# The seven-product form for all eight chunk pairs of an up group, and one panel of the down rounds added up in its banks

## The chip, the cores and the metric

One core of one Trainium2 chip runs the kernel. The metric is device time in microseconds (us) of one execution. The engines of the core work side by side and wait for each other by semaphores: TensorE (PE, matmuls; PEld is its loading of stationary operands), VectorE (DVE), ScalarE (ACT), GpSimd (POOL) and SyncE (SP). SP and POOL issue DMAs, each in the order of its own program. On the chip matmuls write into eight PSUM banks; here a bank holds a tile of 128 rows and 512 columns.

## What is computed

One layer of a streaming encoder for 256 frames of a new stream and 8 x 16 frames of running streams: 384 tokens, in three tiles of 128 (tiles 0 and 1 are the new stream, tile 2 the running ones). The change concerns the last part, the feed-forward block:

```python
h2 = rmsnorm(x, norm_ffn_g)
up = h2 @ w_up                       # 2048 -> 2 x 5632
g_half, u_half = up[..., :D_FF], up[..., D_FF:]
ext_f = concatenate([ffn_buf, g_half], axis=1)
gc = causal_dwconv(ext_f, ffn_dw_w, ffn_dw_b)      # 3 taps along the frames
x = x + (silu(gc) * u_half) @ w_down               # 5632 -> 2048
new_ffn = ext_f[:, -2:]
```

All inputs and outputs are float32.

## The kernel before

Each float32 operand of a matmul is split into a high half (a copy rounded to the matmul's type, made by ACT: `hi`) and a low half (the rest, a subtraction on DVE: `lo`). A product of a 128 x 128 block of tokens and a 128 x 512 block of weights is three matmuls into one bank: high by high, high by low, low by high (`three`). The tokens are the stationary operand. The weights come by SP as loads of 512 KB, two chunks of 128 rows by 512 columns each, into streaming buffers (`raw`, and `raws`, two more in a tile that is free by then: five in all).

Up to the output projection the program runs in `gemm`. The feed-forward part goes by `FFN_PLAN`: 11 groups of 512 columns of the inner width. An up group g makes the gate and value rows of its columns; a down round multiplies the group's activation into four panels of 512 output columns, 2 steps of 18 matmuls each, and adds each panel's three banks into `y` on DVE. Up group g+1 runs ahead of the down round of group g. Group 0 is plain (`plain_up`, 288 matmuls). Groups 1 to 10 run in `wino`, with 16 chunks of the 2048 inputs taken as 8 pairs. For a pair with chunks c0 and c1, tokens x0 (tile 0) and x1 (tile 1), gate weights G0, G1 and value weights U0, U1, the eight products of the 2 x 2 block product are done as seven, with four combinations of tokens (`sums`, made once per layer) and four of weights, made on DVE for every pair:

- S1 = U0 - G0, S2 = U0 - U1, S3 = U1 - S1, S4 = G1 - S3

Tile 2 takes four plain products, with one sum of tokens so that it can share S2. That is 11 products a pair in place of 12. In the kernel before, pairs 0 to 5 run so and pairs 6 and 7 (chunks 12 to 15) run plainly: 6 x 11 + 2 x 12 = 90 products. The steps (`WINO_STEPS`) are "s" (gate weights as loaded, 12 matmuls), "b" (the U1 of two pairs, 12 matmuls), "t" (the combined weights, two splits with 9 and 6 matmuls; gate and value weights of the pair are loaded for it, the gate weights a second time), and "cg", "cu" (plain pairs, 18 matmuls): 270 matmuls, 25 splits and 25 loads a group.

The order of the work around a step is set by a planner inside the program, when the program is built. `step` puts down one step: it issues ACT's high half of the split that is next in `staged`, the row work that the step before released (`fins`), the matmuls, the low half on DVE, and the sums for the next pair (`combine`). Row work of earlier groups waits in `todo` and is put down by `work` whenever the planner's clock (`now`, with a cost per operation) says that an engine has time. The engines then run exactly that order. Two splits are prepared ahead of the step that PE works on (`ready`), in three pairs of tiles.

`finish_up` is the row work of a group: gate and value rows come out of the banks (`rows_from` on ACT, `rows_plus` on DVE), are turned in blocks (DVE, into `tb`), moved by SP and POOL into `uT`, and then run through the conv taps (`sg`), SiLU and product into the split activation `act`. `norm_panel`, ahead of the feed-forward part, turns and splits the normalized tokens into `xg` and makes the `sums`.

## Time and profile before

| | |
|---|---|
| three timed runs, median (lowest to highest) | 1957.12 us (1957.06 to 1957.96) |
| the profiled execution | 1957.32 us, its span 1955.6 us |
| granted clock of TensorE | 1.00 |
| feed-forward part | from 908.2 us to the end |
| HBM read | 314 MB, 165 GB/s over the span with the writes |

A row of the timeline has the start and the duration in us, the engine, the line of the program, the operation, what it writes and reads with its shape, and a count; in brackets stands the idle time of the engine in front of it and what ended that. All calls that the planner issues for DVE, ACT, POOL and SP have one line, that of a helper (L1112), so such rows are told apart by their tiles. A row of the groups by line has count, busy time in all, mean duration in ns, idle time in front and what ended it.

### The profile page before, as it was taken

Reading aid. Unit: us, or ns where it says so; the run is one execution under the profiler, and the core shown is the slowest. Engines: PE = TensorE matmul, PEld = TensorE weight load, DVE = VectorE, ACT = ScalarE, POOL = GpSimd, SP = SyncE. Lnnn points to the kernel's source line nnn. Section 1 sums busy time; section 2 is a strip of 40 time slices with the busy share of each in tenths; the row PEclk is TensorE's granted clock in tenths of the full one; section 3 lists DMA queues with packets and bytes.
Section 4 is the critical chain, followed back from the end, with each engine's and each line's share of the span. In section 5 each row is a group of like instructions: output and inputs, shape, how many; then the busy total and the mean of one; then the engine's idle time right before and its main releaser. Section 6 shows DMA issues by size and latency. Waiting matters only on the chain.

```text
span 1955.6 us, 25545 instructions
## 1 busy us (share of the span) xinstructions
PE 1945.8 (99%) x9192; PEld 1639.0 (84%) x9192; DVE 1478.2 (76%) x2016; ACT 878.3 (45%) x1220; POOL 150.8 (8%) x298
## 2 busy tenths in 40 slices
PE   9999999999999999999999999999999999999999
PEld 9888999988888888888888888888887888888887
DVE  4456979888764578677587878787878787878885
ACT  5535454433333523344454444454444444454552
POOL 2000011100000000000111010101010101010110
PEclk9999999999999999999999999999999999999999
DMA  6574777554444333644576666666666666667664
GB/s 188 149 184 118 221 169 154 146 141 134 131 131 126 122 129 119 201 133 139 155 218 203 198 203 200 201 203 197 207 191 205 195 213 191 207 192 217 209 185 141
DMA packets 245203, 340.58 MB, mean 174 GB/s; under 512 B 60794, under 2 KB 106549, under 8 KB 245067
## 3 DMA queue, kind: packets, MB, share of 16 engines
q1 hardware_dynamic: 237875, 328.93, 56.9%
q0 software_dynamic: 7168, 10.00, 1.9%
q8 instruction: 72, 1.18, 0.3%
q14 instruction: 56, 0.46, 0.1%
q10 hardware_dynamic: 32, 0.01, 0.0%
HBM read 314.17 MB, written 7.86 MB: 165 GB/s over the span
## 4 chain that ended last, share of the span: by engine, by line
PE 93%; DVE 4%; issue 1%; ACT 1%; DMA 1%; SPq 0%; ACTq 0%; DVEq 0%
PE bank L1368 16%; PE bank L1369 16%; PE bank L1367 16%; PE acc L325 8%; PE acc L323 8%; PE acc L324 8%; PE misc L325 4%; PE misc L323 4%; PE misc L324 4%; PE acc L318 2%; PE acc L320 2%; PE acc L319 2%; DVE lo L1112 1%; DVE raw L1112 1%; ACT hi L1112 1%
## 5 line engine op out<-in xcount | busy, mean ns | idle before, releaser
L175 DVE TENSOR_TENSOR lo<-raw,hi 128x1024 fp32r<-128x1024 f32 (+2 forms) x219 | 259.9, 1188 | 196.1 <-ACT hi L174 193.9
L174 ACT CAST hi<-raw 128x1024 fp32r<-128x1024 f32 (+2 forms) x219 | 221.6, 1012 | 391.6 <-PE misc L325 305.4
L1112 ACT CAST hi<-raw 128x1024 fp32r<-128x1024 f32 x215 | 225.7, 1050 | 319.7 <-PE bank L1369 268.9
L1112 DVE TENSOR_TENSOR lo<-raw,hi 128x1024 fp32r<-128x1024 f32 x215 | 262.0, 1221 | 86.4 <-ACT hi L1112 83.2
L1368 PE MATMUL bank<-lo,xg 128*128 128x512 f32 x656 | 256.4, 391 | 1.6 <-DVE lo L1112 1.6
L1367 PE MATMUL bank<-hi,xg 128*128 128x512 f32 x656 | 255.3, 389 | 0.0
L1369 PE MATMUL bank<-hi,xg 128*128 128x512 f32 x656 | 255.3, 389 | 0.0
L1112 ACT CAST hi<-raws 128x1024 fp32r<-128x1024 f32 x137 | 144.4, 1054 | 201.6 <-PE bank L1369 166.4
L1112 DVE TENSOR_TENSOR lo<-raws,hi 128x1024 fp32r<-128x1024 f32 x137 | 167.3, 1222 | 64.4 <-ACT hi L1112 62.2
L1368 PE MATMUL bank<-lo,act 128*128 128x512 f32 x528 | 205.6, 389 | 0.0
L1369 PE MATMUL bank<-hi,act 128*128 128x512 f32 x528 | 205.4, 389 | 0.0
L1367 PE MATMUL bank<-hi,act 128*128 128x512 f32 x528 | 205.4, 389 | 0.0
L323 PE MATMUL acc<-hi,hT 128*128 128x512 f32 (+1 forms) x512 | 192.9, 377 | 0.0
L325 PE MATMUL acc<-hi,hT 128*128 128x512 f32 (+1 forms) x512 | 190.4, 372 | 0.1
L324 PE MATMUL acc<-lo,hT 128*128 128x512 f32 (+1 forms) x512 | 190.3, 372 | 0.2 <-DVE lo L175 0.2
L840 DVE SCALAR_TENSOR_TENSOR ut<-ext,cw,ut 128x384 f32<-128x384 f32 x240 | 151.3, 630 | 6.0
L1368 PEld LDWEIGHTS bank<-lo,xg 128*128 128x128 f32 x656 | 123.1, 188 | 31.0 <-DVE lo L1112 5.8
L1112 POOL DMA_DIRECT2D uT<-tb x168 | 82.8, 500 | 855.5 <-DVE y L1112 640.7
L1367 PEld LDWEIGHTS bank<-hi,xg 128*128 128x128 f32 x656 | 123.1, 188 | 25.9
L1369 PEld LDWEIGHTS bank<-hi,xg 128*128 128x128 f32 x656 | 123.2, 188 | 25.3
L1368 PEld LDWEIGHTS bank<-lo,act 128*128 128x128 f32 x528 | 99.1, 188 | 21.1 <-DVE lo L1112 0.6
L1367 PEld LDWEIGHTS bank<-hi,act 128*128 128x128 f32 x528 | 99.1, 188 | 20.6
(355 smaller groups left out, 3620.2 us busy)
## 6 DMA issues: line engine op xcount, KB each, us to landing
raw<-in_w_up_dram SPq DMA_DIRECT2D x161, 512.0 KB
raws<-in_w_up_dram SPq DMA_DIRECT2D x105, 512.0 KB
raw<-in_w_in_dram SPq DMA_DIRECT2D x96, 512.0 KB
raw<-in_w_down_dram SPq DMA_DIRECT2D x56, 512.0 KB
raw<-in_w_in_dram SPq DMA_DIRECT2D x64, 256.0 KB
raw<-in_w_out_dram SPq DMA_DIRECT2D x32, 512.0 KB
raws<-in_w_down_dram SPq DMA_DIRECT2D x32, 512.0 KB
raw<-in_w_att_out_dram SPq DMA_DIRECT2D x16, 512.0 KB
```

Source lines behind the costliest of these rows:

```text
L174: queued(nc.scalar.copy(hi[:, k, :o], raw[:, k, :o]), first)
L175: queued(tt(lo[:, k, :o], raw[:, k, :o], f(hi[:, k, :o]), op=ALU.subtract), first)
L318: mm(o, hi[:, kk, s], ah, start=st, stop=False)
L319: mm(o, hi[:, kk, s], al, start=False, stop=False)
L323: mm(o, ah[:, s], hi[:, kk, :n], start=st, stop=False)
L324: mm(o, ah[:, s], lo[:, kk, :n], start=False, stop=False)
L325: mm(o, al[:, s], hi[:, kk, :n], start=False, stop=sp)
L840: stt(o, v, wc, o, op0=ALU.mult, op1=ALU.add)
L1112: d = op(*args, **kw)
L1367: mm(o, ah, h[:, kk, :], start=start, stop=False, **kw)
L1368: mm(o, ah, l[:, kk, :], start=False, stop=False, **kw)
L1369: mm(o, al, h[:, kk, :], start=False, stop=stop, **kw)
```

## The change

- The eight pairs of groups 1 to 10 all take the seven-product form. Each pair's gate and value weights are loaded once (entry "Q" of the plan), and the pair has three splits: A (gate weights as loaded, 12 matmuls), B (S2 and U1, 12) and C (S1 and S4, 6). S3 of the pair goes to a tile of its own (`t2`, in the tiles `tb`, `ur` and `sg`, which are free at that time), and the S3 of all pairs are used at the end of the group in four steps of two pairs (D, 6 matmuls each). A group has 264 matmuls, 28 splits (one of the D splits in two pieces) and 16 loads.
- A fourth pair of tiles for splits (`wide`): the tile of tokens that only group 0 reads is used for it afterwards, and a step without matmuls ahead of group 1 makes one split more stand ready: three ahead.
- Four streaming buffers in place of five. The plan runs each down round in one piece.
- Panel 2 of each down round (`SEEDED`): ACT copies the three tiles of y into the banks ahead of the panel, the matmuls add to them, and ACT copies the sums back into y. The other panels are added on DVE as before.
- Gate rows are finished first; the value rows of two banks are made by DVE behind the turning of the gate rows, and turned into the tile of the gate rows. `norm_panel` lays the tokens out by tile and makes the sums of all four panels.
- The planner's costs for a low half and a sum are smaller (1.05 and 0.6 in place of 1.22 and 0.7), and it looks at DVE, ACT and SP in turns until nothing more fits (`settle`).

```diff
     def stream_tile():
-        made[2] += made[2] % 5 == 4 and made[3]
-        i = made[2] % 5 if banks else 0
+        i = made[2] % 4 if banks else 0
...
     def split_tiles():
+        if banks and wide[0]:
+            wide[0] += 1
+            if wide[0] % 4 == 1:
+                return res["wide"]()
...
-    FFN_PLAN += [("up", 9), ("down", (8,), range(3)), ("up", 10), ("down", (8,), range(3, 4)), ("down", (9,)), ("down", (10,))]
+    FFN_PLAN += [("up", 9), ("down", (8,)), ("up", 10), ("down", (9,)), ("down", (10,))]
...
+        res["x21"] = [p_xg.tile([P, 8, P], F32R, tag=tag, bufs=1, name=tag) for tag in ("x21h", "x21l")]
+        res["wide"] = lambda: [p_xg.tile([P, 2, 512], F32R, tag=tag, bufs=1, name=tag) for tag in ("x21h", "x21l")]
...
+        parts = [(*(xg[:, i, 0:8].rearrange("p (m t) i -> p m t i", t=2) for i in range(2)),
+                  yT[:].rearrange("p m (t i) -> p m t i", t=NTT)[:, :, 0:3:2]),
+                 (xg[:, 0, 8:10], xg[:, 1, 8:10], x[:, :, 1, 1]), (*x21, x[:, :, 0, 1])]
+        for hi, lo, v in parts:
+            nc.scalar.copy(hi, v)
+        for hi, lo, v in parts:
+            tt(lo, v, f(hi), op=ALU.subtract)
...
-    MM, HI, LO, SUM, RAWS = 0.227, 1.05, 1.22, 0.7, 5
+    MM, HI, LO, SUM, RAWS = 0.227, 1.05, 1.05, 0.6, 4
...
+                rg, ru = raw_tile(), raw_tile()
+                load(rg, e[3])
+                load(ru, e[4])
+                for k in e[2]:
+                    staged.append(("D",) + k if k[0] not in ABC else {"A": ("A", rg), "B": ("B", ru, rg, e[1]),
+                                                                        "C": ("C", rg, ru, e[1])}[k])
...
     def combine(e):
+        _, ru, rg, i = e
+        t, o = t2(i)
+        t = t[:, o:o + 512]
+        V.tensor_tensor(rg[:, 0, :], ru[:, 0, :], rg[:, 0, :], op=ALU.subtract)
+        V.tensor_tensor(ru[:, 0, :], ru[:, 0, :], ru[:, 1, :], op=ALU.subtract)
+        V.tensor_tensor(t, ru[:, 1, :], rg[:, 0, :], op=ALU.subtract)
+        V.tensor_tensor(rg[:, 1, :], rg[:, 1, :], t, op=ALU.subtract)
...
     def wino(g):
+            if k == "A":
                 steps.append([[(tok(2 * i, 0), 1), (tok(2 * i, 2), "g")], [(tok(2 * i + 1, 0), 2), (tok(2 * i + 1, 2), "g")]])
+            elif k == "B":
+                steps.append([[(summed(2, i), 7), (tok(2 * i, 2), "u")], [(summed(3, i), 3), (summed(4, i), "u")]])
+            elif k == "C":
+                steps.append([[(summed(0, i), 5)], [(tok(2 * i + 1, 1), 4)]])
             else:
+                steps.append([[(summed(1, i), 1)] for i in k])
...
+        def one(t):
+            bs.append(take())
+            A.copy(bs[-1][1][:], rows_of(t, n))
...
-                    V.tensor_tensor(ys, ps[:], ys, op=ALU.add)
+                    if n in SEEDED:
+                        A.copy(ys, ps[:])
+                    else:
+                        V.tensor_tensor(ys, ps[:], ys, op=ALU.add)
...
+            if not wide[0]:
+                wide[0] = 4
+                load_ahead(0.0)
+                step(0, lambda h, l: ready.insert(0, (h, l)))
             wino(g)
```

How the order moves on two engines. First DVE in the middle of an up group, before: a "t" step's sums and its two splits, with a "c" step's split between them (`raw_12751` and `raws` hold the pair's weights, `lo_12813` is the "c" step's).

```order
L1112 TENSOR_TENSOR raw_12751<-raws_7690,raw_12751 128x512
L1112 TENSOR_TENSOR raws_7690<-raws_7690 128x512
L1112 TENSOR_TENSOR raws_7690<-raws_7690,raw_12751 128x512
L1112 TENSOR_TENSOR lo_12793<-raws_7690,hi_12792 128x1024
L1112 TENSOR_TENSOR raw_12751<-raw_12751,raws_7690 128x512
L1112 TENSOR_TENSOR lo_12813<-raws_7690,hi_12812 128x1024
L1112 TENSOR_TENSOR lo_12827<-raw_12751,hi_12826 128x1024
```

DVE at the same place after the change: one pair (`raw_10642` the gate weights, `raw_10643` the value weights, `t2_10587` the tile of S3).

```order
L1103 TENSOR_TENSOR lo_10674<-raw_10642,hi_10673 128x1024
L1103 TENSOR_TENSOR raw_10642<-raw_10643,raw_10642 128x512
L1103 TENSOR_TENSOR raw_10643<-raw_10643 128x512
L1103 TENSOR_TENSOR t2_10587<-raw_10643,raw_10642 128x512
L1103 TENSOR_TENSOR raw_10642<-raw_10642,t2_10587 128x512
L1103 TENSOR_TENSOR lo_10697<-raw_10643,hi_10696 128x1024
L1103 TENSOR_TENSOR act3_10568<-uT_10380,act3_10568 128x4x6x32
L1103 TENSOR_TENSOR lo_10713<-raw_10642,hi_10712 128x1024
```

The low half of the gate weights (A) now stands ahead of the sums, because the sums overwrite what it reads; all four sums stand in one piece, and the low halves of B and C follow, with a piece of the earlier group's row work between them.

Then ACT at the end of an up group, before: the last splits of the group, the value rows out of the banks (`ur`), and the first splits of the down round.

```order
L1112 CAST hi_10054<-raws_7690 128x1024
L1112 ACTIVATE ur_10057<-bank_9690,rs2_6845 128x512
L1112 CAST hi_10071<-raws_7690 128x1024
L1112 CAST hi_10082<-raw_10012 128x1024
L1112 CAST hi_10097<-raw_10025 128x1024
L1112 ACTIVATE ur_10057<-bank_9831,rs2_6845 128x512
L1112 ACTIVATE ur_10057<-bank_9694,rs2_6845 128x512
L1112 CAST hi_10113<-raw_10052 128x1024
```

After the change: the D splits, which read `t2`, with the gate rows (`gr`) and the value rows of three banks, and then the first split of the down round (`hi_10890`).

```order
L1103 CAST hi_10825<-t2_10587 128x1024
L1103 CAST hi_10843<-t2_10368 128x512
L1103 CAST hi_10843<-t2_10587 128x512
L1103 ACTIVATE gr_10847<-bank_10464,rs2_6847 128x512
L1103 ACTIVATE gr_10847<-bank_10468,rs2_6847 128x512
L1103 CAST x21h_10865<-t2_10368 128x1024
L1103 ACTIVATE ur_10868<-bank_10489,rs2_6847 128x512
L1103 ACTIVATE ur_10868<-bank_10493,rs2_6847 128x512
L1103 ACTIVATE ur_10868<-bank_10497,rs2_6847 128x512
L1103 CAST hi_10879<-t2_10739 128x1024
L1103 CAST hi_10890<-raw_10764 128x1024
```

Five rows out of banks now stand between the four splits of the D steps, where three stood among the splits of the last steps before.

More of the change, by code (lines that the diff above doesn't have):

```diff
@@ L1231, in step @@
         products(h, l)
-        if staged:
+        if nxt:
+            if slack[0] > 1:
+                work("DVE", max(hi_done + 0.1, end - 0.5))
+            else:
+                settle(hi_done + 0.1, max(hi_done + 0.1, end - 1.2 if mults == 18 else 0.0))
+            now["DVE"] = max(now["DVE"], hi_done) + LO
+            with tc.high_priority(offset=high):
+                for k, x in pieces(nxt):
+                    V.tensor_tensor(lo[:, k], x, f(hi[:, k]), op=ALU.subtract)
+            ready.append((hi, lo))
+            if nxt[0] not in ("A", "D"):
+                room.append(now["DVE"])
@@ L1233, in step @@
+        if staged and staged[0][0] == "B" and staged[0] is not formed[0]:
             with tc.high_priority(offset=high):
                 combine(staged[0])
-        if nxt:
-            work("DVE", max(hi_done + 0.1, end - 0.5 if slack[0] > 1 else 0.0))
-            now["DVE"] = max(now["DVE"], hi_done) + LO
-            with tc.high_priority(offset=high):
-                V.tensor_tensor(lo[:], nxt[1][:], f(hi[:]), op=ALU.subtract)
-            ready.append((hi, lo))
-            room[0] += 1
+        settle(end + slack[0], end + slack[0])
```

337 lines of the change are left out of this document (178 added, 159 removed).

## The prediction, made before the run

> **What bounds the kernel now.** First the page: the span, the busy shares, and the chain that ended last.
>
> ```profile
> span 1955.6 us, 25545 instructions
> PE 1945.8 (99%) x9192; PEld 1639.0 (84%) x9192; DVE 1478.2 (76%) x2016; ACT 878.3 (45%) x1220; POOL 150.8 (8%) x298
> ...
> PE 93%; DVE 4%; issue 1%; ACT 1%; DMA 1%; SPq 0%; ACTq 0%; DVEq 0%
> ```
>
> TensorE (PE) is busy all the time and makes up 93% of the chain, so the end is set by how many matmuls there are, at what distance they follow each other, and how often PE has to wait. The profiled execution took 1957.3 us, 1.7 us more than its span and 0.2 us more than the median of the three timed runs; I add to and take from 1957.3.
>
> A matmul's duration is no use for that, since matmuls overlap. The distance I take from the timeline of one down round: its first matmul and the first of the up group behind it, 144 matmuls later.
>
> ```profile
> 1602.54 0.39 PE L1367 MATMUL bank<-hi,act 128*128 128x512 f32 x1
> ...
> 1635.18 0.39 PE L1367 MATMUL bank<-hi,xg 128*128 128x512 f32 x1
> ```
>
> 32.64 us by 144 is 0.2267 us for one, and nothing was lost there. The next view is busy time by stage: one up group (270 matmuls) and the down round behind it. The columns are the stretch, its length, then busy time of PE, weight loads, DVE, ACT and POOL with counts, the clock, the DMA share and GB/s.
>
> ```profile
> 1540.89:1602.54 61.65, 61.49 (x272) 50.61 (x270) 52.46 (x61) 31.12 (x33) 0.00 (x0) 1.00 0.66 200
> 1602.54:1635.18 32.64, 32.64 (x146) 27.04 (x144) 25.36 (x34) 13.89 (x20) 9.47 (x19) 1.00 0.71 204
> ```
>
> 270 matmuls at 0.2267 are 61.20 us, so an up group loses 0.45 us today. The view of waits names what PE waits for in the whole feed-forward part:
>
> ```profile
> PE bank L1368 <- DVE lo L1112: 2.6, 12, 0.7
> ```
>
> Twelve waits for a low half made by VectorE (DVE), 2.6 us seen. What matters for the change is thus how much work DVE can still take inside an up group: it is busy for 52.46 of 61.65 us.
>
> **The PE term.** Per group 6 pairs of chunks cost 11 products today and 2 pairs cost 12: 90. Afterwards 8 pairs cost 11: 88. A product is three matmuls, so a group has 264 in place of 270; the ten groups lose 60, and the listing has PE rows 8802 before and 8742 after. 60 x 0.2267 = **13.6 us less**. The matmuls have the same shape, and the granted clock is 1.00 throughout. If nothing new waits, the time is 1957.3 - 13.6 = 1943.7.
>
> **What DVE gets in exchange.** The groups of the round above (one up group, one down round), by line; the last column is idle time before them and what ended it:
>
> ```profile
> L1112 DVE TENSOR_TENSOR lo<-raw,hi 128x1024 fp32r<-128x1024 f32 x20 | 24.4, 1222 | 7.7 <-ACT hi L1112 7.2
> L1112 DVE TENSOR_TENSOR lo<-raws,hi 128x1024 fp32r<-128x1024 f32 x13 | 15.9, 1222 | 5.1 <-ACT hi L1112 4.8
> L1112 DVE TENSOR_TENSOR raw<-raw 128x512 f32<-128x512 f32 x13 | 9.0, 689 | 0.8 <-DMA raw<-in_w_up_dram 0.6
> L1112 DVE TENSOR_TENSOR y<-bank,y 128x512 f32<-128x512 f32 x13 | 8.3, 678 | 0.4 <-PE bank L1369 0.4
> ...
> L1112 DVE SCALAR_TENSOR_TENSOR sg<-extf,fw,sg 128x384 f32<-128x384 f32 x9 | 5.2, 612 | 0.0
> ...
> L1112 DVE SCALAR_TENSOR_TENSOR gr<-bank,rs,gr 128x512 f32<-128x512 f32 x1 | 0.8, 751 | 0.4 <-PE bank L1369 0.4
> ```
>
> A group goes from 25 low halves to 27 whole ones and two of half size, from 24 sums and differences of weights to 32, and gets one more addition out of a bank; a down round gives three of its twelve additions into y to ScalarE (ACT). 2 x 1.22 + 2 x 0.69 (at most; half of 1.22 is 0.61) + 8 x 0.69 + 0.75 - 3 x 0.68 = 8.1 us more. DVE's 77.8 us in a round of 94.3 become 85.9 in 92.9, 92%. The average still fits; the up group is what has to be checked.
>
> The order repeats a piece of DVE work for each pair: four sums, three low halves. The same mix runs today, where a "t" step is followed by a "c" step, and the timeline shows what it takes when DVE is pressed:
>
> ```profile
> 1565.98 0.69 DVE L1112 TENSOR_TENSOR raw<-raws,raw 128x512 f32<-128x512 f32 x1
> 1566.70 0.69 DVE L1112 TENSOR_TENSOR raws<-raws 128x512 f32<-128x512 f32 x1
> 1567.43 0.69 DVE L1112 TENSOR_TENSOR raws<-raws,raw 128x512 f32<-128x512 f32 x1
> 1568.04 1.22 DVE L1112 TENSOR_TENSOR lo<-raws,hi 128x1024 fp32r<-128x1024 f32 x1
> 1569.17 0.69 DVE L1112 TENSOR_TENSOR raw<-raw,raws 128x512 f32<-128x512 f32 x1
> 1569.77 1.22 DVE L1112 TENSOR_TENSOR lo<-raws,hi 128x1024 fp32r<-128x1024 f32 x1
> 1571.11 1.23 DVE L1112 TENSOR_TENSOR lo<-raw,hi 128x1024 fp32r<-128x1024 f32 x1
> 1572.87 0.69 DVE L1112 TENSOR_TENSOR raws<-raw,raws 128x512 f32<-128x512 f32 x1 [0.53 <-DMA raws<-in_w_up_dram]
> ```
>
> The starts matter: a low half keeps DVE for 1.13 us before the next one may start (1568.04 to 1569.17), not for its 1.22, and from 1565.98 to the time at which the next piece could start without the load, some 0.1 us before 1571.11 + 1.23, are **6.3 us**, a wait of 0.2 us for ACT's high half included (1569.77 to 1571.11). A pair now gives PE 30 matmuls in its steps A, B and C, 6.80 us. So DVE gains 0.5 us a pair, and uses it for the rest.
>
> Sum for one up group, PE time 264 x 0.2267 = 59.8 us. Pairs: 8 x 6.3 = 50.4. The four D steps: three low halves and two of half size, at most 5.0. Row work that the order puts here: one conv tap 0.61, three additions into y 1.9, four operations on halves of the activation at 0.95 (row 1914.10 below), two gate rows 1.5: 7.8. In all 63.2. But the order prepares three splits ahead of PE (before: two), so the first pair's 6.3 us are done in the down round, and at the end one split (1.22) must be ready for the next stage: 58.1 of 59.8. **DVE keeps 1.7 us a group.** In the down round it has even more room: 85.9 - 63.2 = 22.7 us of work in 32.6.
>
> A low half starts its follower 0.09 us before its own end (1.13 of 1.22). The Trainium skill speaks against this and against any change that adds operations: by its page "VectorE: DVE Perf Modes", section "The DRAIN you can't avoid", the next operation does not start until the pipe is empty. The rows above differ, and the measurement decides; what the time would be without that overlap stands among the rivals.
>
> **ACT.** Its high halves and row work of the round:
>
> ```profile
> L1112 ACT CAST hi<-raw 128x1024 fp32r<-128x1024 f32 x20 | 21.0, 1051 | 31.3 <-PE bank L1369 28.0 <-DVE lo L1112 1.7 <-ACT act L1112 0.9
> ...
> L1112 ACT ACTIVATE ur<-bank,rs 128x512 f32<-128x512 f32 x3 | 1.9, 679 | 0.0
> L1112 ACT COPY extf<-uT 128x384 f32<-128x384 f32 x4 | 1.8, 517 | 0.0
> ```
>
> It gets the same additional splits (two whole, two half) and six copies between bank and y. No such copy runs in this form today: between the 0.52 us of a smaller copy and the 0.68 of a row out of a bank; I take 0.65, the nearer shape. +7.1 us, 45 becomes 52 of 92.9. ACT's idle time ends mostly with PE (28.0 of 31.3: it waits for a buffer), so it has room on average. The narrow place is the edge of a group, where step B of the last pair completes three banks at once. From there to step D3, 1.36 + 3 x 1.36 = 5.4 us, ACT makes a high half, three rows and another high half in front of DVE's low half: 1.05 + 3 x 0.63 + 1.05 + 1.22 = 5.2 us, and with some tenths between engines that is just late. I price the edge at 0 to 0.5 us a group and take today's 0.45, which the deeper preparation otherwise removes: **no change in PE's waits**. Gone altogether they would be worth 10 x 0.45 = 4.5 us.
>
> **Loads.** 25 loads of 512 KB a group become 16 (the gate weights of a pair were loaded twice), but five buffers become four.
>
> ```profile
> DVE raw L1112 <- DMA raw<-in_w_up_dram: 9.3, 11, 2.2
> DVE raws L1112 <- DMA raws<-in_w_up_dram: 6.2, 9, 1.7
> ```
>
> Over nine rounds DVE waited 20 times for a load, at most 2.2 us. Bounds: none of it left (1.7 us a round gained for DVE, nothing for the end) to one wait of 2.2 a group, 0.5 beyond DVE's 1.7. I take nothing.
>
> **Both ends.** At the start of the feed-forward part norm_panel(3) makes some 2 us more of small operations. Its low half is the first row here, PE's first matmul of the part the second:
>
> ```profile
> 926.89 1.76 DVE L1037 TENSOR_TENSOR xg<-yT,xg 128x1536 fp32r<-128x1536 f32 x1
> ...
> 908.21 0.39 PE L1367 MATMUL bank<-hi,xg 128*128 128x512 f32 x1
> ```
>
> Its first use is 108 matmuls in, at 932.7; it is done at 928.7, so 2 us cost nothing.
>
> At the other end, group 10's activation had the last panel of round 8 and all of round 9 in front of the round that needs it: 180 matmuls, now 144, 8.2 us less cover. The rows are PE's first matmul behind group 10, the turning of its gate rows, DVE's first product with the gates, the first low half of the activation, PE's first matmul of the last round, and the second low half:
>
> ```profile
> 1877.30 0.39 PE L1367 MATMUL bank<-hi,act 128*128 128x512 f32 x1
> ...
> 1883.50 1.89 DVE L1112 STREAM_TRANSPOSE tb<-gr 128x512 f32<-128x512 f32 x3
> ...
> 1910.15 0.96 DVE L1112 TENSOR_TENSOR uT<-uT,sg 128x768 f32<-128x768 f32 x1 [3.68 <-DMA raw<-in_w_down_dram]
> ...
> 1914.10 0.95 DVE L1112 TENSOR_TENSOR act<-uT,act 128x768 fp32r<-128x768 f32 x1
> ...
> 1918.21 0.39 PE L1367 MATMUL bank<-hi,act 128*128 128x512 f32 x1
> ...
> 1920.43 0.95 DVE L1112 TENSOR_TENSOR act<-uT,act 128x768 fp32r<-128x768 f32 x1
> ```
>
> The first half was done 37.8 us after the group (1915.05), the second 44.1 us (1921.38, inside the round's first step). Now they are needed after 32.6 and 36.7: a chain as long as today's would cost up to 7.4 us. But it starts earlier. The gate rows were turned by 1885.4, 8.1 us after the group, behind five rows out of banks; now they stand behind one gate row and one low half, and can be done 0.75 + 1.13 + 1.89 = 3.8 us after it. The rest of today's chain waited too: DVE stood idle for 3.7 us ahead of the product at 1910.15. Between 0 and 7.4 I take 0, the end that the 4.3 us at the start and the 3.7 us of waiting are nearer to.
>
> **Sum.** 1957.3 - 13.6 + 0 (edges, loads, ends) = 1943.7; I forecast **1944**.
>
> **Rivals.** *VectorE gets late in the up groups (slower).* Mechanism: each split waits for its high half, which ACT can make only after DVE's sums. Today's row has 7.2 + 4.8 us of such idle time on 33 splits, 0.36 each. With that on 27 splits, 9.7 us in place of the 1.6 that the 6.3 hold, DVE is 9.7 - 1.6 - 1.7 = 6.4 us late per group, and ten groups end at 1944 + 64 = 2008. It decides from 0.17 us a split on, where the gain is used up (10 x 1.36). For it: DVE at 92%, ACT fuller. Against: ACT itself waits for PE's buffers in 28.0 of 31.3 us, so today's idle time is slack; where DVE was pressed, one wait in three was 0.2. Chance 0.13, anywhere from 1953 to 2008, more than half of it above 1961.
>
> *Edges and the end cost (less gain).* 0.5 us more at each edge and up to 7.4 at the end: 1944 + 5 to 12, so 1949 to 1956. Chance 0.17.
>
> *VectorE's operations follow each other without overlap (less gain).* Then a pair takes 3 x 1.22 + 4 x 0.69 + 0.2 = 6.6 us, the up group 8 x 6.6 + 12.8 - 6.6 + 1.2 = 60.2 of 59.8, and ten groups are late by 4 us: 1948, with 0.5 us more at each edge 1953. Against it stand the starts at 1568.04 and 1569.17. Chance 0.03. This is what the Trainium skill's rule named above would do here.
>
> *The deeper preparation takes today's waits too (more gain).* 1943.7 - 4.5 = 1939. For it: today's waits come with two prepared splits; against: the D steps are as short as the ones that wait today. Chance 0.15.
>
> *The change doesn't do what it says.* The count of matmuls is certain from the listing; it has no chance of its own.
>
> **How the numbers follow.** Forecast 0.52 (1940 to 1949), more gain 0.15, less gain 0.17 + 0.03, late DVE 0.13. A difference of 0.2% (3.9 us) is about what a measurement of this kernel can tell, so faster is below 1953.2 and slower above 1961.0. Faster: 0.52 + 0.15 + 0.12 of the less gain = 0.79; same: 0.08 of the less gain and 0.05 of the late DVE = 0.13; slower: 0.08. The range goes from 1938 (all edge waits gone, and a us of other waits with them) to 1955; it leaves out the late DVE and the worst of the less gain.
>
> **What would show it.** PE rows 60 fewer and the down rounds still 32.64 us; up groups of 59.8 to 60.4 us. DVE some 83 to 86 us busy in a round of 92.5 to 93, its waits for high halves no longer than today's. If the up groups take over 61.2, DVE or ACT got late: then PE's waits name a low half in the middle of a group (DVE), at D3 or the first down step (ACT at the edge), or a bank. If the loss is at the end, PE waits ahead of the last round for the activation. The prediction is wrong if PE's waits grow past 13.6 us.

## The result, and the profile after

The changed kernel takes **1939.28 us** (median of 5 runs, 1938.59 to 1940.24) against 1957.12 (5 runs, 1956.54 to 1958.2): a ratio of 0.9907, 95% interval 0.9893 to 0.9922. That is 17.8 us less; forecast were 13.6, from 1957.3 to 1943.7, given as 1944 in a range from 1938 to 1955. The profiled execution took 1940.24 us, 17.1 less than the one of before.

The page of the changed kernel: its span, the busy shares, and the engines' shares of the chain that ended last.

```profile
span 1938.5 us, 25431 instructions
PE 1929.1 (100%) x9132; PEld 1628.5 (84%) x9132; DVE 1552.2 (80%) x2125; ACT 938.7 (48%) x1334; POOL 151.6 (8%) x298
...
PE 96%; DVE 2%; DMA 1%; SPq 0%; ACT 0%; issue 0%; ACTq 0%; DVEq 0%
```

TensorE (PE) has 60 matmuls fewer and makes up still more of the chain. The view by stage shows where the time went: an up group and the down round behind it (stretch, length, then busy time of PE, weight loads, VectorE, ScalarE, POOL with counts, clock, DMA share, GB/s).

```profile
1345.19:1405.03 59.84, 59.84 (x265) 49.55 (x264) 55.67 (x65) 34.48 (x38) 0.00 (x0) 1.00 0.42 141
1405.03:1437.67 32.64, 32.64 (x145) 27.03 (x144) 29.41 (x40) 16.10 (x25) 9.52 (x19) 1.00 0.60 179
```

264 matmuls at 0.2267 us are 59.85 us, so this group (group 5) loses nothing, and the down round is 32.64 us as before. To set all kernels side by side I take from each trace the distance from the first matmul of a stage to the first of the next, less the number of matmuls times 0.2267: the time that PE lost in the stage, in us.

```
kernel             groups 1 to 10                                               sum     round of group 9
before             0.46 0.99 0.46 0.45 0.45 1.48 0.44 0.48 0.44 0.44             6.1    0.11
after              0.00 in each                                                  0.0    1.17
b_lowfirst         1.02 11.22 14.18 12.95 14.41 12.96 14.39 12.98 14.18 13.85  122.1    0.00
b_gate_step_first  1.42 0.66 0.68 0.66 0.62 0.65 0.66 0.63 0.71 0.64             7.3    0.00
a_two_ahead        4.86 3.52 4.86 3.51 3.58 3.48 5.38 3.76 3.46 4.75            41.2    0.39
a_sums_first       1.32 1.51 1.51 1.48 1.76 1.47 1.47 1.50 1.50 1.47            15.0    1.47
a_two_sums_first   12.66 11.26 12.84 12.83 12.93 12.43 11.26 12.83 12.69 11.27 123.0    0.00
a_edge_row         0.61 0.61 0.61 0.61 0.61 1.04 1.04 1.04 1.04 1.04             8.3    1.21
a_three_sums_more  1.55, then 0.03 at most                                       1.7    1.30
a_all_sums_more    4.45 3.53 3.53 3.90 3.54 3.54 3.54 3.55 3.53 3.53            37.1    0.72
a_no_seeds         0.00 in each                                                  0.0    0.00
a_round9_added     0.00 in each                                                  0.0    0.00
a_again            0.00 in each                                                  0.0    1.52
a_round9_last      0.00 in each                                                  0.0    0.00
```

The 17.1 us between the two profiled executions are thus 13.6 for the 60 matmuls and 6.1 for waits in the groups that are gone; against these 19.7 stand 0.8 at the end (the new 1.17 us in the round of group 9, less 0.11 there and 0.26 in the last round before) and 1.8 ahead of the feed-forward part. Most of that last item is a wait of 1.3 us in code that the change leaves alone (`PE acc L318 <- ACT hT L378` in the view of waits). It varies from execution to execution: over the eleven profiles of the changed kernel and its variants the part began between 908.43 and 909.99 us, over the three of before and its variants between 908.21 and 908.75.

Of TensorE's waits in the feed-forward part one is left:

```profile
PE bank L1410 <- ACT bank L1103: 0.9, 1, 0.9
```

The timeline of ScalarE (ACT) shows its making (start, length, and in brackets idle time before it and what ended it):

```profile
1883.18 1.05 ACT L1103 CAST x21h<-raw 128x1024 fp32r<-128x1024 f32 x1 [2.25 <-DMA raw<-in_w_down_dram]
1884.13 1.62 ACT L1103 COPY bank<-y 128x512 f32<-128x512 f32 x3
```

The three copies of y into the banks that the next panel adds to stand behind a high half that waits 2.25 us for its load. ScalarE does its work in order, so PE waits for copies that stand behind that load; two runs below test it by moving or leaving out the copies.

### The profile page after: what moved, and what is told of

It reads as the page before. It is cut to its first block, busy times and chain, and to the rows that moved or that the text cites. A ratio compares the mean times of both kernels' runs of the same rounds, so it can differ in the third digit from the quotient of the medians.

```text
span 1938.5 us, 25431 instructions
## 1 busy us (share of the span) xinstructions
PE 1929.1 (100%) x9132; PEld 1628.5 (84%) x9132; DVE 1552.2 (80%) x2125; ACT 938.7 (48%) x1334; POOL 151.6 (8%) x298
## 4 chain that ended last, share of the span: by engine, by line
PE 96%; DVE 2%; DMA 1%; SPq 0%; ACT 0%; issue 0%; ACTq 0%; DVEq 0%
PE bank L1410 17%; PE bank L1411 17%; PE bank L1412 17%; PE acc L320 8%; PE acc L318 8%; PE acc L319 8%; PE misc L320 4%; PE misc L319 4%; PE misc L318 4%; PE acc L313 2%; PE acc L315 2%; PE acc L314 2%; DMA raw<-in_w_in_dram 0%; DVE mixT L337 0%; DVE lo L177 0%
## 5 line engine op out<-in xcount | busy, mean ns | idle before, releaser
L1103 DVE TENSOR_TENSOR lo<-raw,hi 128x1024 fp32r<-128x1024 f32 x260 | 314.5, 1219 | 50.3 <-ACT hi L1103 48.7
L318 PE MATMUL acc<-hi,hT 128*128 128x512 f32 (+1 forms) x512 | 192.9, 377 | 1.3 <-ACT hT L378 1.3
L1410 PE MATMUL bank<-hi,xg 128*128 128x512 f32 x440 | 171.2, 389 | 0.0
L1411 PE MATMUL bank<-lo,xg 128*128 128x512 f32 x440 | 171.2, 389 | 0.0
L1412 PE MATMUL bank<-hi,xg 128*128 128x512 f32 x440 | 171.2, 389 | 0.0
L1410 PE MATMUL bank<-hi,act 128*128 128x512 f32 x396 | 154.2, 389 | 0.9 <-ACT bank L1103 0.9
L1412 PE MATMUL bank<-hi,act 128*128 128x512 f32 x396 | 154.1, 389 | 0.0
L1411 PE MATMUL bank<-lo,act 128*128 128x512 f32 x396 | 154.1, 389 | 0.0
L1103 ACT CAST x21h<-raw 128x1024 fp32r<-128x1024 f32 x82 | 86.2, 1052 | 101.4 <-DVE raw L1103 50.0
L318 PEld LDWEIGHTS acc<-hi,hT 128*128 128x128 f32 x512 | 96.3, 188 | 16.7 <-ACT hT L378 1.8
L320 PEld LDWEIGHTS acc<-hi,hT 128*128 128x128 f32 x512 | 96.1, 188 | 15.9 <-DVE hT L379 0.9
L319 PEld LDWEIGHTS acc<-lo,hT 128*128 128x128 f32 x512 | 96.2, 188 | 15.3 <-DVE lo L177 0.5
L1103 DVE TENSOR_TENSOR x21l<-raw,x21h 128x1024 fp32r<-128x1024 f32 x82 | 100.1, 1220 | 7.6 <-ACT x21h L1103 6.4
L1410 PEld LDWEIGHTS bank<-hi,xg 128*128 128x128 f32 x440 | 82.6, 188 | 17.2
L1411 PEld LDWEIGHTS bank<-lo,xg 128*128 128x128 f32 x440 | 82.6, 188 | 17.1
L1412 PEld LDWEIGHTS bank<-hi,xg 128*128 128x128 f32 x440 | 82.6, 188 | 17.1
```

The lines of the kernel that those rows point to most:

```text
L318: mm(o, ah[:, s], hi[:, kk, :n], start=st, stop=False)
L319: mm(o, ah[:, s], lo[:, kk, :n], start=False, stop=False)
L320: mm(o, al[:, s], hi[:, kk, :n], start=False, stop=sp)
L1103: d = op(*args, **kw)
L1410: mm(o, ah, h[:, kk, :], start=start, stop=False, **kw)
L1411: mm(o, ah, l[:, kk, :], start=False, stop=False, **kw)
```

## The experiments

**Why did the old waits go?** The prediction named the edge of the group as the narrow place, priced it at 0.45 us a group and so left the waits of before in the sum. The timelines of before show where they lie. VectorE (DVE), in group 5:

```profile
1376.35 2.14 DVE L1112 TENSOR_TENSOR raws<-raws 128x512 f32<-128x512 f32 x3
1378.41 1.22 DVE L1112 TENSOR_TENSOR lo<-raw,hi 128x1024 fp32r<-128x1024 f32 x1
```

And TensorE at that time:

```profile
1379.14 0.39 PE L1367 MATMUL bank<-hi,xg 128*128 128x512 f32 x1
1379.68 0.50 PE L1368 MATMUL bank<-lo,xg 128*128 128x512 f32 x1 [0.16 <-DVE lo L1112]
```

The low half of the first "cg" step ends at 1379.63 behind three sums, and PE's second matmul of that step, the first to read it, starts at 1379.68. This is the middle of the group (it began at 1351.26), not its edge. Every group from 1 to 10 loses 0.45 to 0.47 us in this step, and eight of them lose nothing else. Groups 2 and 6 lose 0.55 and 1.01 us more in the first "cu" step, for another reason: a load. VectorE waits 1.67 us for weights in group 2 and 2.16 in group 6; in group 6 these are the weights of the third "t" pair,

```profile
1479.17 0.69 DVE L1112 TENSOR_TENSOR raw<-raws,raw 128x512 f32<-128x512 f32 x1 [2.16 <-DMA raw<-in_w_up_dram]
```

and TensorE then for the low half behind those sums, which the "cu" step uses:

```profile
1482.50 0.50 PE L1368 MATMUL bank<-lo,late 128*128 128x512 f32 x1 [0.72 <-DVE lo L1112]
```

So of the 6.1 us in the table 4.5 are the wait at the "cg" step and 1.6 are late loads in this execution. After the change VectorE waits for no load of up weights, and with two splits ahead (a_two_ahead) it doesn't either, so that isn't the depth. The 16 loads a group in place of 25 are the likely reason; the number of loads was not changed by itself.

The 4.5 us at the "cg" step are the question of the next runs. (In the chapter on the change the low half of the "c" step is the first in the excerpt, `lo_12793` behind the three sums, not `lo_12813`.) Two theories follow: **depth** (two prepared splits are too few; the change prepares three) and **order** (the low half stands behind the next pair's sums; the change puts that of step A ahead of them). One run turns the order round in the kernel before:

```diff
-        if staged:
+        if staged and (t < 140):
             with tc.high_priority(offset=high):
                 combine(staged[0])
...
             ready.append((hi, lo))
             room[0] += 1
+        if staged and not (t < 140):
+            combine(staged[0])
```

> The kernel before, with one thing altered: in groups 2 to 10 and their down rounds the low half of a step is issued to VectorE ahead of the sums for the next pair, not behind them. Order theory (today's waits of about 0.45 us a group came from the low half of the first gate step of the plain pairs standing behind three sums): the up groups 2 to 10 take 61.20 us in place of 61.65 and more, 5 us less in all. Depth theory (two prepared splits are too few, whatever the order): the groups stay at 61.65 us, 0 us.

2073.47 us against 1956.58 on the same chip: the order theory falls, and in this kernel the order that I suspected is the one that keeps it fast. The view of waits (us in total, times, longest) has for DVE, in before:

```profile
DVE lo L1112 <- ACT hi L1112: 145.4, 135, 2.9
```

and for ACT, in before:

```profile
ACT hi L1112 <- DVE raw L1112: 22.9, 25, 1.7
```

With the low half first it has for DVE:

```profile
DVE lo L1112 <- ACT hi L1112: 275.8, 232, 2.9
```

and for ACT:

```profile
ACT hi L1112 <- DVE raw L1112: 180.9, 69, 4.5
```

A low half at the head of DVE's queue waits for its high half, while sums that could be made stand behind it; then ACT's next high half waits for those sums. Sums first, DVE fills the time in which ACT makes the high half.

The other half of the question, in the changed kernel: two splits ahead in place of three,

```diff
-            if not wide[0]:
-                wide[0] = 4
-                load_ahead(0.0)
-                step(0, lambda h, l: ready.insert(0, (h, l)))
```

the sums ahead of step A's low half,

```diff
         products(h, l)
+        if staged and staged[0][0] == "B" and staged[0] is not formed[0]:
+            with tc.high_priority(offset=high):
+                combine(staged[0])
         if nxt:
...
-        if staged and staged[0][0] == "B" and staged[0] is not formed[0]:
-            with tc.high_priority(offset=high):
-                combine(staged[0])
```

and both. In the last two the sums overwrite gate weights that step A's low half still reads, so that half is made of altered weights; the operations, their number and their shapes are those of the change.

> The changed kernel without the fourth buffer pair for splits: two splits are prepared ahead of TensorE in place of three. Depth theory: each up group loses at least the 0.45 us that it lost before the change, ten groups 4.5 us or more, and most of it at the last D step, where with three ahead the split is done 0.06 us before it is needed. Order theory: the groups stay at 59.84 us but for the edge, 0 to 1 us in all.

> The changed kernel, with the four sums for the next pair put ahead of the low half of step A on VectorE, as the order of before had them; three splits are prepared ahead as in the change. Depth theory: 59.84 us a group as in the change, 0 us. Order theory: the low half of A is 2.5 us later in each pair; where it was done less than 2.5 us ahead of its use (it is 2.8 to 4.2 us ahead in the middle of a group), PE waits, so up to 0.5 us a group, 5 us in all.

> The changed kernel with both undone: two splits ahead, and the four sums ahead of the low half of step A. Both theories expect waits here: the depth theory as many as with two ahead alone (4.5 us or more in all), the order theory 0.45 us a group or more above that, since a low half that is 2.5 us later meets a lead that is one split shorter.

Measured: 1979.62, 1954.32 and 2061.6 us, 41, 15 and 123 us lost in the groups. Depth is worth far more than the 4.5 us expected: without the third split the changed kernel is slower than the one before (1956.58). DVE's timeline shows a first part of what the third split does; one pair in group 5 with two ahead:

```profile
1401.65 0.69 DVE L1103 TENSOR_TENSOR raw<-raw,raw 128x512 f32<-128x512 f32 x1
...
1404.31 2.49 DVE L1103 TENSOR_TENSOR lo<-raw,hi 128x1024 fp32r<-128x1024 f32 x2
1406.72 0.95 DVE L1103 TENSOR_TENSOR act<-uT,act 128x768 fp32r<-128x768 f32 x1
1407.59 1.22 DVE L1103 TENSOR_TENSOR lo<-raw,hi 128x1024 fp32r<-128x1024 f32 x1
1408.85 1.42 DVE L1103 TENSOR_TENSOR raw<-raw 128x512 f32<-128x512 f32 x2
```

From the first sum of a pair to the first of the next are 7.20 us, of which 0.87 is row work, with no idle time; PE needs 6.80 for the pair. The changed kernel has the same pair in 7.07 us (rows in the next section). So in the middle of a group DVE is slower than PE, with two splits ahead as with three, and only work done ahead covers it. How far ahead is the lead below: from the end of a split's low half to PE's first matmul of the step that uses it, us, group 5, both times from the trace. The low half is first read by the step's second matmul, 0.23 us later; below about -0.2 PE waits for it. A wait ahead of the first matmul doesn't show here.

```
                    A0    A2    A4    A6    B6    D1    D2    D3
after              9.69  3.97  3.30  2.76  1.55  1.48  1.57  0.06
a_two_ahead        5.65  1.46  0.90  0.78 -0.42  0.57 -1.21  0.16
a_three_sums_more  9.69  3.95  2.54  1.29  0.09  1.42  1.57  0.01
a_all_sums_more    9.69  3.22  1.63  0.93 -1.00  0.82  1.04 -0.60
a_edge_row         9.69  4.25  4.04  4.25  1.42  1.47  0.83 -0.66
```

With three ahead the group starts with 9.69 us of lead, uses 8.1 of it by step B of the seventh pair (B6), and no step waits. With two it starts with 5.65, and is used up at the fourth pair: waits of 0.3 to 0.4 at step B of the later pairs. The larger part of the loss stands at the edge, though: over the ten groups 14 us at the B steps and 27 at the D steps. In group 5 TensorE waits twice at D2, 0.9 us ahead of its first matmul and 1.1 at its second:

```profile
1420.43 0.50 PE L1410 MATMUL bank<-hi,sums 128*128 128x512 f32 x1 [0.77 <-ACT hi L1103]
1421.69 0.50 PE L1411 MATMUL bank<-lo,sums 128*128 128x512 f32 x1 [0.76 <-DVE lo L1103]
```

ScalarE makes the high half of D2 behind the three value rows there:

```profile
1417.60 1.84 ACT L1103 ACTIVATE ur<-bank,rs 128x512 f32<-128x512 f32 x3 [0.84 <-DVE lo L1103]
1419.32 2.00 ACT L1103 CAST hi<-t 128x1024 fp32r<-128x1024 f32 x2
```

With three ahead it makes it in front of them (in the changed kernel's group 5 at 1398.43, the rows from 1399.57 on):

```profile
1398.43 1.05 ACT L1103 CAST x21h<-t 128x1024 fp32r<-128x1024 f32 x1 [0.36 <-PE bank L1412]
```

So the third split buys lead on VectorE in the middle of the group and puts one more split in front of ScalarE's rows at its end. The order of the sums matters in the changed kernel too (15 us, all at the A steps), and there low half first is right. Depth and order together are no sum (123, not 41 + 15).

To see the old wait from the other side, the steps of before in another order, the long gate step ahead of the first pair (the end of the list `WINO_STEPS`):

```diff
-("b", 4), ("t", 0), ("cg", 12), ("t", 1), ("cu", 12), ("t", 2), ("cg", 14), ("t", 3), ("cu", 14), ("t", 4), ("t", 5)]
+("b", 4), ("cg", 12), ("t", 0), ("cu", 12), ("t", 1), ("cg", 14), ("t", 2), ("cu", 14), ("t", 3), ("t", 4), ("t", 5)]
```

> The kernel before, with the first step of the plain pairs (18 matmuls, gates of chunks 12 and 13) put ahead of the first pair of the seven-product form with shared weights, and so on alternately: the same steps, in another order. Lead theory (the wait of 0.45 us in the middle of each group stands where the first sums and splits of such a pair meet a lead of two short steps, 9 and 6 matmuls): with a long step ahead of it the wait goes, 61.20 us a group, some 5 to 6 us less in all. Rival (two prepared splits are too few for the mix wherever it stands): 61.65 us or more.

1960.05 us (before: 1958.47), 61.83 us in group 5: no gain (and the last round loses 1.36 us, before 0.26). The wait at the first gate step is gone, as the lead theory said, but PE's timeline has waits at two other places, where the last pairs follow each other with short steps alone:

```profile
1409.28 0.39 PE L1367 MATMUL bank<-hi,late 128*128 128x512 f32 x1
1409.63 0.50 PE L1368 MATMUL bank<-lo,late 128*128 128x512 f32 x1
...
1410.90 0.40 PE L1367 MATMUL bank<-hi,late 128*128 128x512 f32 x1
1411.37 0.50 PE L1368 MATMUL bank<-lo,late 128*128 128x512 f32 x1
```

0.35 and 0.47 us between matmuls in place of 0.23. The mechanism holds (a lead of short steps is too short for the mix), the gain doesn't: with two ahead the wait moves. Three ahead in the kernel before was not tried; that depth alone would take its 4.5 us away is thus argued from the changed kernel, not shown. Nor were the planner's new costs, its turns (`settle`) and the four streaming buffers tried by themselves.

**Is the edge as narrow as forecast?** One row of ScalarE at the edge, made twice:

```diff
-                             7: lambda: [rows_from(7, ur, 1)], "u": lambda: [rows_from("u", ur, 2)],
+                             7: lambda: [rows_from(7, ur, 1)] * 2, "u": lambda: [rows_from("u", ur, 2)],
```

> The changed kernel with one row out of a bank done twice by ScalarE at the edge of each group (the copy of bank 7's middle row block, 0.63 us, between step B of the last pair and step D3); the result is the same. Edge theory (ScalarE's high halves and rows there take 5.2 of 5.4 us, and step D3's split is done 0.06 us ahead of its use): each group loses 0.63 - 0.06 = 0.57 us at D3, 5.7 us in ten groups. Rival (the edge is set by TensorE's banks or by VectorE, and ScalarE has room): 0 to 1 us in all.

1948.81 us; 0.61 in each of the first five groups and 1.04 in the others, 8.3 in all, the whole at D3. The timeline of the changed kernel itself, group 5, for ScalarE:

```profile
1399.57 1.85 ACT L1103 ACTIVATE ur<-bank,rs 128x512 f32<-128x512 f32 x3
1401.30 1.05 ACT L1103 CAST hi<-t 128x1024 fp32r<-128x1024 f32 x1
```

for VectorE:

```profile
1402.38 1.23 DVE L1103 TENSOR_TENSOR lo<-t,hi 128x1024 fp32r<-128x1024 f32 x1 [0.98 <-ACT hi L1103]
```

and for PE, the first matmul of step D3:

```profile
1403.67 0.39 PE L1410 MATMUL bank<-hi,late 128*128 128x512 f32 x1
```

The low half is done at 1403.61, 0.06 us ahead of step D3 and 0.29 ahead of the matmul that reads it first. DVE itself waits 0.98 us there for ScalarE: the edge is ScalarE's, and it fits with little to spare. From group 6 on, ScalarE's timeline in a_edge_row shows a wait ahead of the rows, which group 5 doesn't have (group 6):

```profile
1495.41 2.57 ACT L1103 ACTIVATE ur<-bank,rs 128x512 f32<-128x512 f32 x4 [0.52 <-DVE lo L1103]
```

These rows start 3.67 us ahead of step D3, in group 5 they start 4.10 ahead. The 0.43 us between them are the difference of 1.04 and 0.61.

**How much room does DVE have?** A sum of three pairs, and of all eight, made twice:

```diff
         V.tensor_tensor(t, ru[:, 1, :], rg[:, 0, :], op=ALU.subtract)
+        if i in (1, 3, 5):
+            V.tensor_tensor(t, ru[:, 1, :], rg[:, 0, :], op=ALU.subtract)
```

> The changed kernel with the third sum of pairs 1, 3 and 5 made twice, 3 x 0.72 = 2.2 us more for VectorE in each up group; the result is the same. Room as the prediction has it (1.7 us a group): 0.4 to 0.7 us lost in each group, 4 to 7 us in all, in the middle of the group from step B of pair 4 on. Rival (VectorE is idle for 4.2 of the group's 59.84 us and can take it all): 59.84 us a group, 0 us in all.

> The changed kernel with the third sum of all eight pairs made twice, 8 x 0.72 = 5.8 us more for VectorE in each up group; the result is the same. With 1.7 us of room (the prediction): 4.1 us lost in each group, 41 us in all. With all of the 4.2 us that VectorE is idle in an up group: 1.6 us lost in each, 16 us in all. Either way the waits stand at step B of the later pairs, since the lead of three splits is eaten up step by step.

1940.62 and 1976.05 us. 2.2 us more cost 1.55 in group 1 and nothing from group 2 on, but bring the lead at B6 down to 0.09; 5.8 more cost 3.54 in most groups (3.0 of it at the B steps, the rest at D3). So there is room for about 5.8 - 3.54 = 2.3 us: neither the 1.7 of the prediction nor all of the idle time. The timeline of VectorE with all eight sums doubled gives the price of one: from 1395.39 to 1396.84 are 1.45 us for two, 0.73 each.

```profile
1395.39 1.41 DVE L1103 TENSOR_TENSOR t<-raw 128x512 f32<-128x512 f32 x2
1396.84 0.69 DVE L1103 TENSOR_TENSOR raw<-raw,t 128x512 f32<-128x512 f32 x1
```

**What is the panel in ScalarE's banks worth?** Without it:

```diff
-    SEEDED = (2,)
+    SEEDED = ()
```

> The changed kernel without the panel that is added up in banks filled by ScalarE: VectorE makes all twelve additions into y in each down round, 3 x 0.68 = 2 us more for it. If that relief is needed to win back the lead of three splits in the down round: each group loses up to 2 us, 20 us in all. If VectorE's idle time in the down round (32.64 - 29.13 = 3.5 us) is enough: 0 us in the groups, and some 1.2 us less for the wait of those copies in the round of group 9.

1938.18 us in one run, nothing lost in any group, and the wait in the round of group 9 gone. In the view by stage, group 5, VectorE's busy time goes from 55.67 to 57.41 us:

```profile
1344.33:1404.17 59.84, 59.84 (x266) 49.55 (x264) 57.41 (x68) 34.59 (x38) 0.00 (x0) 1.00 0.45 141
```

The relief is not needed: the down round wins the lead back without it (9.74 us at A0). In this one run the part of the change brings nothing, and leaving it out takes the wait of 1.17 us away.

**Can that wait be had back?** Two edits, each for the round of group 9 alone: all four panels added up by VectorE (a_round9_added), or ScalarE's copies for the fourth panel in place of the third:

```diff
-    SEEDED = (2,)
+    def seeded_panel(g):
+        return 3 if g == 9 else 2
...
-                    if n in SEEDED:
+                    if n == seeded_panel(gs[0]):
                         A.copy(ys, ps[:])
```

> The changed kernel, but the third panel of the down round of group 9 is added up by VectorE as the other panels are, with no copies of y into its banks by ScalarE. If the only wait that the change left (1.17 us, where ScalarE's copies into those banks stand behind a high half that waits for its load) comes from that order: 1.2 us less, the round 32.64 us. Rival (the late load itself holds TensorE up, whoever adds): 0 us, the wait moves to the split of that load.

> The changed kernel itself, once more, beside the next run on the same chip: 1939 us. Of the 1.75 us that its first profile lost early in the run, in code that the change doesn't touch: there again if it belongs to the kernel, gone if it belongs to that one execution.

> The changed kernel, but in the down round of group 9 it is the fourth panel, not the third, that is added up in banks filled by ScalarE: the copies of y come some 8 us later, when the loads that were held back for group 10's gates have arrived. If the 1.17 us wait is the copies' place behind the late load: 1.2 us less than the changed kernel, with no wait in round 10 either (VectorE's work stays the same), 1938 us. Rival (something else in round 9 or 10 gets late, as when VectorE added up all four panels, where 0.7 us came back as a wait for the activation in round 10): 0.5 us less at most.

a_round9_added took 1938.18 us (4 runs, 1937.9 to 1938.68; ratio to before 0.9895, interval 0.9879 to 0.9912). The wait is gone, but the last round then loses 0.71 us. The timeline of the changed kernel says why. The first low half of group 10's activation on VectorE:

```profile
1899.73 0.95 DVE L1103 TENSOR_TENSOR act<-uT,act 128x768 fp32r<-128x768 f32 x1
```

and PE's first matmul of the last round:

```profile
1901.24 0.39 PE L1410 MATMUL bank<-hi,act 128*128 128x512 f32 x1
```

The first half is done at 1900.68, 33.25 us after the group (which ended 32.64 + 1.17 = 33.81 ahead of 1901.24, at 1867.43). Without the wait it would be needed after 32.64 and the 0.23 to the second matmul: the 1.17 us hid that it is just too late. In a_round9_added it is done after 33.62. With the copies moved to the fourth panel (a_round9_last) it is done after 32.88 and costs 0.02 us; in a_no_seeds after 31.94, and nothing is lost. So this chain stands within a us of its limit in all of them. On one chip, 1938.01 us (4 runs, 1937.48 to 1938.37; ratio to before 0.9897, interval 0.9882 to 0.9911) stand against 1939.60 for the changed kernel (4 runs, 1939.40 to 1939.65; 0.9905, 0.9888 to 0.9921): **1.6 us less**. By their ratios and ranges, a_round9_last, a_round9_added and a_no_seeds can't be told apart. ScalarE's timeline in a_round9_last shows the copies well after the late load:

```profile
1882.26 1.05 ACT L1104 CAST x21h<-raw 128x1024 fp32r<-128x1024 f32 x1 [1.85 <-DMA raw<-in_w_down_dram]
...
1887.63 1.62 ACT L1104 COPY bank<-y 128x512 f32<-128x512 f32 x3
```

The repeat of the changed kernel began its feed-forward part at 909.04 us (first profile: 909.99; before: 908.21), so about half of the 1.8 us at the start belonged to that one execution; whether some tenths of the rest belong to the change stays open, since the ranges above overlap.

## Why the prediction was right, step by step

- **The PE term**, 60 x 0.2267 = 13.6 us: right. Groups of 59.84, down rounds of 32.64, 13.6 of the 17.1 us.
- **"Take today's 0.45 ... no change in PE's waits"**: this term was mis-sized, at 0; it measured 6.1. The prediction saw that the depth removes the waits of before ("which the deeper preparation otherwise removes") and set a price of 0.45 us a group for the new edge against it. That price was wrong: the edge costs 0. The waits of before were in the middle of the group, ten of 0.45 that went with the depth, as the bound of 10 x 0.45 = 4.5 had them, and 1.6 us of late loads in two groups, which the bound left out. (That depth took the ten away is shown in the changed kernel alone.) The rival "the deeper preparation takes today's waits too", 1939 us at a chance of 0.15, is what happened. That its figure meets the time is luck in part: 1957.3 - 13.6 - 6.1 = 1937.6, and 0.8 at the end and 1.8 ahead of the feed-forward part, which it didn't have, make it 1940.2 for the profiled execution. The prediction had the lead in its sum for VectorE (58.1 of 59.8 with the first pair done ahead), and didn't ask what the same lead does to the waits of before; a_two_ahead shows that it is worth 41 us in this kernel.
- **VectorE's load**: 8.1 us more a round forecast, to 85.9; measured 55.67 + 29.41 = 85.1. Room 1.7 forecast, about 2.3 measured. A pair was forecast at 6.3 us. VectorE's timeline of the changed kernel, one pair in group 5, has 7.07 from 1369.13 to 1376.20, of which 0.87 (1372.94 to 1373.81) is row work: 6.2.

```profile
1369.13 0.69 DVE L1103 TENSOR_TENSOR raw<-raw,raw 128x512 f32<-128x512 f32 x1
1369.86 0.69 DVE L1103 TENSOR_TENSOR raw<-raw 128x512 f32<-128x512 f32 x1
1370.47 0.68 DVE L1103 TENSOR_TENSOR t<-raw,raw 128x512 f32<-128x512 f32 x1
1371.18 0.69 DVE L1103 TENSOR_TENSOR raw<-raw,t 128x512 f32<-128x512 f32 x1
1371.80 1.23 DVE L1103 TENSOR_TENSOR lo<-raw,hi 128x1024 fp32r<-128x1024 f32 x1
1372.94 0.95 DVE L1103 TENSOR_TENSOR act<-uT,act 128x768 fp32r<-128x768 f32 x1
1373.81 1.22 DVE L1103 TENSOR_TENSOR x21l<-raw,x21h 128x1024 fp32r<-128x1024 f32 x1
...
1376.20 1.42 DVE L1103 TENSOR_TENSOR raw<-raw 128x512 f32<-128x512 f32 x2
```

- **Operations without overlap** (1948 to 1953): fell. The operation at 1372.94 starts 0.09 us before the low half at 1371.80 + 1.23 ends. The Trainium skill limits the rule that the prediction named: by its page "VectorE: DVE Perf Modes", section "Two Vector instructions with no wait between them", only an instruction that is held, for where its operands start, begins when every earlier one has finished. These rows agree with that. The section that the prediction drew on points to this limit in its own words, and the prediction left it out.
- **VectorE gets late in the up groups**: fell, by 2.3 us a group. a_all_sums_more shows the price beyond it, 37 us, 31 of them at the place named ("a low half in the middle of a group").
- **The edge**, 5.2 of 5.4 us, 0 to 0.5 lost: it fits by 0.06 us, so 0, where the sum had taken 0.45. The chain itself took 5.18 us (1398.43 to 1403.61), as counted, and the tenths between engines, which were to make it late, came to 0.20; the low half also has 0.23 us more, until the matmul that reads it first. ScalarE's copies from y into the banks, taken at 0.65, take 0.54 (three in 1.62).
- **Loads**, 0: too small. TensorE's 1.6 us behind late loads in groups 2 and 6 are gone, where the prediction had "nothing for the end", and none of VectorE's 20 waits for up weights is left. One late load of down weights costs 1.17 us in the round of group 9.
- **Both ends**, 0: measured 0.8 us at the end. The sum is near, the step is not. At the start nothing was lost to norm_panel(3). At the end the activation's chain (33.25 us in place of 37.8) was covered only by a wait that the prediction didn't see: the copies into the banks were priced by their duration, not by what stands ahead of them in ScalarE's queue.

## What to carry to other kernels

When a producer is slower than its consumer for a part of a round, look at the lead with which that part begins and what it is worth, not only at the averages: here one more pair of prepared buffers (4 us of lead) decided whether the same change wins 17 us or loses 23. A change of depth acts on the waits of the old kernel as well; find each of them in the timeline, not in the totals, and what ended it, before pricing it at "as today". An operation moved onto an engine that works in order costs what its neighbours wait for: see which load or buffer the one ahead of it needs.

## What the runs showed of the chip

Waits of TensorE can cost more than their own length. PE's timeline in b_lowfirst, group 5:

```profile
1454.63 0.40 PE L1371 MATMUL bank<-hi,xg 128*128 128x512 f32 x1
1456.85 0.49 PE L1369 MATMUL bank<-hi,late 128*128 128x512 f32 x1 [1.83 <-ACT hi L1112]
1458.11 0.80 PE L1370 MATMUL bank<-lo,late 128*128 128x512 f32 x1 [0.76 <-DVE lo L1112]
1458.71 0.63 PE L1371 MATMUL bank<-hi,late 128*128 128x512 f32 x1
1459.13 0.63 PE L1369 MATMUL bank<-hi,xg 128*128 128x512 f32 x1
```

Starts are 2.2 and 1.3 us apart there, with one matmul between, and then the matmuls follow each other at 0.42 to 0.43 us in place of 0.227. The view by stage (the third figure from the end is the granted clock) shows that the clock was halved inside the second gap, at 1457.3, for 6.8 us:

```profile
1453.90:1457.30 3.40, 1.57 (x6) 0.75 (x4) 2.09 (x4) 1.54 (x2) 0.00 (x0) 1.00 0.55 178
1457.30:1464.10 6.80, 6.04 (x15) 4.75 (x15) 4.18 (x5) 4.21 (x6) 0.00 (x0) 0.50 0.49 137
```

Counting all such distances, 89 matmuls at 0.2 us more are 17.8 of the 122 us that this run lost (29 and 5.8 of 41 in a_two_ahead). The Trainium skill, page "TensorE: Matmul & The Clock Gate", Part 1, ties the half clock to an idle window of about 3.4 us and gives two states; the two spacings and the clocks of 1.00 and 0.50 here agree with two states. No stretch of 3.4 us without a matmul was needed, though: PE's longest idle time there is 1.83 us, and in the 3.4 us before the clock was halved PE was busy for 1.57. In the changed kernel, which has no such gaps, the granted clock is 1.00.

On VectorE a sum that doesn't need the one before it starts some 0.08 us before that one's end (1369.86 + 0.69 against 1370.47), one that does 0.02 to 0.04 after it (1370.47 + 0.68 against 1371.18): so, as an estimate from these rows, the less chained of two orders of the same sums is shorter by 0.1 us a link; no run here tried it.
